# The two rounds of 32x32 products in a block inverse, spread over four cells of the matrix array

## The chip, the cores and the metric

The kernel runs on one core of a Trainium2 chip. That core has TensorE (PE: matmuls, and PEld for their weight loads), VectorE (DVE), ScalarE (ACT), GpSimd (POOL) and SyncE (SP), which issues the transfers. The metric is device time of one execution in microseconds (us). Before the change three runs took 1629.48 to 1632.38 us, median 1632.25 us.

## The reference: what is computed

The reference is a two-layer encoder trunk of width 1024, applied with one set of weights to a prompt of 512 tokens and a sample of 256. Layer 0 is a Mamba-2 mixer, layer 1 an RWKV-7 time mix; each is followed by a residual sum and a layer norm. The part that matters here is the recurrence of the second layer, for 16 heads of size 64, forward and backward in time:

```python
def step(s, inp):
    r_t, w_t, k_t, v_t, kk_t, a_t = inp
    sa = jnp.einsum('bhvk,bhk->bhv', s, -kk_t)
    s = (s * w_t[:, :, None, :] + sa[..., None] * (kk_t * a_t)[:, :, None, :]
         + v_t[..., None] * k_t[:, :, None, :])
    return s, jnp.einsum('bhvk,bhk->bhv', s, r_t)
```

The kernel doesn't step through the tokens. It takes chunks of 64 tokens. Inside a chunk the rank-one terms `sa` depend on each other through a triangular 64x64 matrix, and the chunk is solved with the inverse of one plus that matrix.

## The kernel before

Everything is float32. The large products are each made of three fp32r matmuls, a high and a low half of each operand (L140, L141, L142); they are called dense matmuls here.

Layer 1 is worked through in 8 blocks `b` of two heads. For each block there are four pieces:

- `rwkv_in(b)`: dense projections of the block's channels (PE, with ACT and DVE shifting and splitting; L737, L739, L122, L123).
- `p1(b)`: from the projections, per window of four chunks, the triangular matrices of the chunks. They land in `TD` (L914). A block has 24 units (6 windows of 4 chunks), and each unit holds two heads: head 0 in partitions 0 to 63, head 1 in 64 to 127.
- `rwkv_inverse(b)`: replaces the triangular matrices by the inverses, described below.
- `chain_step(b, 0..7)`: the eight dependent steps along the sequence, with small 64x64 matmuls (`pr`, `pS`, `pz` at L1017, `py` at L1039). The product `pS` of step 0 is the first to read the inverses.

`rwkv_inverse` treats each 64x64 triangle as 32x32 quarters. The two diagonal quarters of all units and heads are inverted together by forward substitution on VectorE: 30 pairs of a product (L963) and a sum (L964), each needing the one before. Two transposes (L966, L967) then give the inverted diagonal quarters in two layouts, `XN` and `XR`. What remains is the off-diagonal quarter, -2 times a product of three 32x32 matrices. It takes two rounds of 48 matmuls, 24 units by 2 heads:

- Round 1 (L977) multiplies the off-diagonal quarter of `TD` with `XN`. Its operands lie in the first 32 partitions of the head (`q0`), and the result is put in the second 32 (`q1`), so two cells of the array are used: row strip 0 with column strip 1, and row strip 2 with column strip 3. The results lie in the PSUM tile `tl`. ScalarE scales them into `E` in SBUF (L979; the profile names that buffer `TL`). This happens in two groups, units 0 to 15 and then 16 to 23; the second group's matmuls write the same PSUM tile that the first group's copy reads, and stand behind that copy.
- Round 2 (L986) multiplies `E` in `q1` with `XR` in `q1` into PSUM tile `px` at `q0`, again on two cells (row strips 1 and 3).
- ScalarE writes the diagonal quarters into `TD` (L982, four instructions), and the last four copies (L989) bring the off-diagonal quarters from `px` into `TD`, head 0 on VectorE and head 1 on ScalarE, each in two pieces (16 units and 8).

The order of the work isn't that of the code. `arrange` builds the dependencies of the whole program and hands them to a list scheduler with a cost for each instruction; the order it finds on each engine is fixed with ordering edges. A change in one place can therefore move instructions everywhere in the program, in layer 0 too.

Of the kernel before, what the change touches and what calls it, by code (L numbers as in the profile page):

```python
# [18 lines left out]
AF = mybir.ActivationFunctionType  # L19
# [29 lines left out]
def bc(ap, axis, n):  # L49
    a = ap.unsqueeze(axis)  # L50
    s = list(a.shape)
    s[axis] = n
    return a.to_broadcast(s)
# [6 lines left out]
class Trunk:  # L60
# [880 lines left out]
    def rwkv_inverse(self, b):  # L941


        nc = self.nc
        TD, XR, TS, XN = self.TD, self.TC, self.TL, self.XN
        hm = self.halfm
        spans = [(slice(u, u + n), slice(o, o + n)) for u, o, n in self.spans(b)]
        fl = lambda t: t.rearrange("p a b -> p (a b)")
        sw = lambda t: t.rearrange("p a b -> p b a")

        TL = self.pt("s", [P, 32, 32], "tl")
        for us, rs in spans:
            nc.scalar.activation(TL[:, us], TD[:, rs, 0, 0:32], AF.Copy, scale=hm[:, 2:3])
            nc.vector.scalar_tensor_tensor(TL[:, us], TD[:, rs, 0, 32:64], hm[:, 3:4], TL[:, us], op0=ALU.mult, op1=ALU.add)
        nc.vector.memset(TL[:, 24:], 0.0)
        nc.vector.transpose(TS, sw(TL))
        nc.scalar.copy(TL, TS)
        nc.vector.memset(fl(TL)[:, ::33], 1.0)
        tmp = fl(XN)
        for j in range(1, 31):  # L960
            m = 31 - j
            t = tmp[:, 0 : m * j].rearrange("p (a b) -> p a b", b=j)
            nc.vector.tensor_tensor(t, bc(TS[:, j + 1 : 32, j], 2, j), bc(TL[:, j, 0:j], 1, m), op=ALU.mult)  # L963
            nc.vector.tensor_add(TL[:, j + 1 : 32, 0:j], TL[:, j + 1 : 32, 0:j], t)  # L964

        nc.vector.transpose(XN, sw(TL))  # L966
        nc.vector.transpose(XR, TL)  # L967
        XN, XR = sw(XN), sw(XR)
        qs = [(slice(64 * h, 64 * h + 32), slice(64 * h + 32, 64 * h + 64)) for h in range(2)]
        E = TS  # L970
        groups = (slice(0, 16), slice(16, 24))
        place = [o + i for _, o, n in self.spans(b) for i in range(n)]
        ps = TL
        for g in groups:
            for u in range(24)[g]:
                for q0, q1 in qs:
                    nc.tensor.matmul(ps[q1, u, :], TD[q0, place[u], 0, 32:64], XN[q0, u, :], start=True, stop=True)  # L977

            nc.scalar.activation(E[:, g], ps[:, g], AF.Copy, scale=-2.0)  # L979
        for us, rs in spans:  # L980
            for i in range(2):
                nc.scalar.activation(TD[:, rs, 0, 32 * i : 32 * i + 32], XR[:, us], AF.Copy, scale=hm[:, i : i + 1])  # L982
        ps = self.pt("s", [P, 32, 32], "px")
        for u in range(24):
            for q0, q1 in qs:
                nc.tensor.matmul(ps[q0, u, :], E[q1, u, :], XR[q1, u, :], start=True, stop=True)  # L986
        for us, rs in spans:
            for h, (q0, q1) in enumerate(qs):
                (nc.vector.tensor_copy if h == 0 else nc.scalar.copy)(TD[q0, rs, 0, 32:64], ps[q0, us])  # L989

    def sv_load(self, b, step):

# [937 lines left out]
```

## Time and profile before

| | before |
|---|---|
| median of the runs | 1632.25 us |
| the profiled execution's own time | 1634.65 us |
| its span, first to last instruction | 1632.9 us |
| PE, DVE busy share of the span | 93%, 83% |
| PE busy in round 1 and in round 2, all 8 inverses | 24.5 us, 23.2 us |
| layer 1, from its first inverse to its last | 893 to 1549 us of the span |

Times in the views count from the first instruction of the span. An fp32 matmul of this size shows as two records, so 48 matmuls are 96 records. Rows of the timeline give start, length, engine, line, operation, names and the number of records merged.

### The profile page before, as it was taken

The page shows a single profiled execution, that of the slowest core. Times are in us where ns is not written, and L with a number is a line of the kernel's source. Part 1 is how long each engine was busy: PE and PEld are TensorE (multiplying, and loading weights), DVE is VectorE, ACT ScalarE, POOL GpSimd, SP SyncE. Part 2 cuts the span into 40 slices and gives each one's busy share as a digit, 9 for nine tenths or more (in the row PEclk, how much of TensorE's full clock was granted, in tenths as well). Part 3 has the DMA queues.
Part 4 walks back from the last instruction along what each step waited for, and adds up shares of the span by engine and source line. Part 5 has one row for each costly group of instructions (what it writes and reads, how often), then busy time and mean ns, then how long its engine had stood idle before and what let it go on. Part 6 is the DMA issues. An engine that isn't in the chain of part 4 may idle for free. (4 is left out here: it accounts for less than half of the span.)

```text
span 1632.9 us, 39446 instructions
## 1 busy us (share of the span) xinstructions
PE 1526.4 (93%) x15210; PEld 1293.0 (79%) x15210; DVE 1361.9 (83%) x3031; ACT 850.8 (52%) x1980; POOL 723.5 (44%) x1007
## 2 busy tenths in 40 slices
PE   7999999999999899999979989999898999988996
PEld 6888888888988689998758767777777777776885
DVE  6779988888888885668688898989989898989768
ACT  4345444544545352424464757657574757656332
POOL 1168465574574661000070836446372836547210
PEclk9999999999999899999988898999899999979998
DMA  5110211212112044513334343443434344354332
GB/s 175 54 47 26 78 40 59 72 65 72 56 36 85 13 143 143 182 53 110 120 109 132 94 122 107 116 140 101 139 88 126 113 121 126 102 159 137 97 111 85
DMA packets 150316, 161.41 MB, mean 99 GB/s; under 512 B 39632, under 2 KB 106928, under 8 KB 150128
## 3 DMA queue, kind: packets, MB, share of 16 engines
q1 hardware_dynamic: 150128, 158.89, 32.5%
q8 instruction: 120, 1.97, 0.5%
q14 instruction: 68, 0.56, 0.1%
HBM read 121.43 MB, written 40.55 MB: 99 GB/s over the span
## 5 line engine op out<-in xcount | busy, mean ns | idle before, releaser
L140 PE MATMUL pj<-xh,whi 128*128 128x256 f32 (+1 forms) x1056 | 384.7, 365 | 18.9 <-ACT whi L122 10.2
L142 PE MATMUL pj<-xh,wlo 128*128 128x256 f32 (+1 forms) x1056 | 381.1, 361 | 4.3 <-DVE wlo L123 4.3
L141 PE MATMUL pj<-xl,whi 128*128 128x256 f32 (+1 forms) x1056 | 378.3, 358 | 1.4 <-DVE xl L136 1.4
L140 PEld LDWEIGHTS pj<-xh,whi 128*128 128x128 f32 x1056 | 207.0, 196 | 50.6 <-ACT whi L122 10.3
L142 PEld LDWEIGHTS pj<-xh,wlo 128*128 128x128 f32 x1056 | 207.3, 196 | 30.6 <-DVE wlo L123 6.2
L141 PEld LDWEIGHTS pj<-xl,whi 128*128 128x128 f32 x1056 | 207.7, 197 | 27.0 <-DVE xl L136 2.0
L122 ACT CAST whi<-wraw 128x512 fp32r<-128x512 f32 x213 | 131.4, 620 | 125.2 <-PE pj L141 61.7
L123 DVE TENSOR_TENSOR wlo<-wraw,whi 128x512 fp32r<-128x512 f32 x213 | 159.9, 755 | 33.3 <-ACT whi L122 31.1
L414 POOL TENSOR_SCALAR G<-past,ddt,dt 128x128 f32<-128x128 f32 x192 | 136.2, 720 | 84.6 <-DVE ddt L320 57.8
L140 PE MATMUL po<-whi,xh 128*128 128x256 f32 x528 | 151.8, 288 | 1.5 <-DVE acc L501 1.5
L142 PE MATMUL po<-whi,xl 128*128 128x256 f32 x528 | 152.0, 288 | 0.0
L141 PE MATMUL po<-wlo,xh 128*128 128x256 f32 x528 | 151.5, 287 | 0.0
L234 DVE SCALAR_TENSOR_TENSOR conv<-conv,convw 128x770 f32<-128x770 f32 x128 | 140.7, 1099 | 1.3
L140 PE MATMUL pz<-whi,xh 128*128 128x256 f32 x384 | 113.9, 297 | 1.1 <-DVE sz L258 1.1
L378 POOL TENSOR_TENSOR xw<-xB,dtws 128x256 f32<-128x256 f32 x64 | 53.5, 845 | 135.8 <-ACT xB L366 126.3
L901 POOL TENSOR_TENSOR G<-EP,Wr 64x256 f32<-64x256 f32 x96 | 88.5, 922 | 56.7 <-DMA Wr<-ind 36.3
L142 PE MATMUL pz<-whi,xl 128*128 128x256 f32 x384 | 111.5, 290 | 0.0
L141 PE MATMUL pz<-wlo,xh 128*128 128x256 f32 x384 | 111.1, 290 | 0.0
L140 PEld LDWEIGHTS po<-whi,xh 128*128 128x128 f32 x528 | 100.8, 191 | 2.9 <-DVE acc L501 1.9
L141 PEld LDWEIGHTS po<-wlo,xh 128*128 128x128 f32 x528 | 100.9, 191 | 1.5 <-issue 0.3
L142 PEld LDWEIGHTS po<-whi,xl 128*128 128x128 f32 x528 | 100.6, 191 | 1.5 <-DVE xl L136 0.2
L903 POOL TENSOR_TENSOR G<-EP,Wr 64x256 f32<-64x256 f32 x96 | 89.4, 931 | 1.7 <-ACT KB L919 0.8
(274 smaller groups left out, 3837.9 us busy)
## 6 DMA issues: line engine op xcount, KB each, us to landing
wraw<-in_r_w_in SPq DMA_DIRECT2D x72, 256.0 KB
Wr<-ind SPq DMA_DIRECT2D x48, 384.0 KB
wraw<-in_m_w_xbc SPq DMA_DIRECT2D x64, 256.0 KB
wraw<-in_m_w_z SPq DMA_DIRECT2D x32, 256.0 KB
wraw<-in_m_w_out SPq DMA_DIRECT2D x32, 256.0 KB
ydram<-yst SPq DMA_DIRECT2D x16, 384.0 KB
yraw<-ydram SPq DMA_DIRECT2D x24, 256.0 KB
ind<-k SPq DMA_DIRECT2D x32, 192.0 KB
```

Source lines behind the costliest of these rows:

```text
L122: nc.scalar.copy(hi, raw)
L123: nc.vector.tensor_sub(lo, raw, hi.bitcast(F32))
L140: mm(ps, ah, bh, start=first, stop=False)
L141: mm(ps, ah, bl, start=False, stop=False)
L142: mm(ps, al, bh, start=False, stop=last)
L234: nc.vector.scalar_tensor_tensor(acc, u[:, t : t + n], w[:, b, t : t + 1], acc, op0=ALU.mult, op1=ALU.add)
L378: nc.gpsimd.tensor_tensor(hv(xw), hv(xB[c][:, 0:256]), bc(self.dtws[:, c, z, hs], 2, 64), op=ALU.mult)
L414: nc.gpsimd.tensor_scalar(G[:, h, :], self.past, self.ddt[:, c, i : i + 1], self.dt[:, c, 0, i : i + 1], op0=ALU.mult, op1=ALU.add)
L901: nc.gpsimd.tensor_tensor(G[hr, ps4, h, 0, :], EP[hr, :, 0:C], w4(tok(W[hr, h])), op=ALU.mult)
L903: nc.gpsimd.tensor_tensor(rho[..., ::-1] if z else rho, EP[hr, :, 1:], w4(tok(W[hr, 2])), op=ALU.mult)
```

## The change

Units 16 to 23 use another column strip than units 0 to 15. In round 1 their results land in `q0` where the others land in `q1`; in round 2 the other way round. The row strips stay, so each row strip now serves two neighbouring cells, one with 16 units and one with 8. The units are issued in the order 0, 16, 1, 2, 17, 3, ... (`mixed`).

Round 1 is one group now, followed by the copies. `E` is read in `q1` by round 2, so the copy of units 16 to 23 must bring them from `q0` to `q1`: it becomes two ScalarE copies of 32 partitions (one per head) in place of one of 128. That is 8 ScalarE instructions more over the 8 inverses. The last four copies keep their number and sizes; for units 16 to 23 they read `q1`.

```diff
-        groups = (slice(0, 16), slice(16, 24))
+        mixed = [u for i in range(8) for u in (2 * i, 16 + i, 2 * i + 1)]
         place = [o + i for _, o, n in self.spans(b) for i in range(n)]
         ps = TL
-        for g in groups:
-            for u in range(24)[g]:
-                for q0, q1 in qs:
-                    nc.tensor.matmul(ps[q1, u, :], TD[q0, place[u], 0, 32:64], XN[q0, u, :], start=True, stop=True)
-
-            nc.scalar.activation(E[:, g], ps[:, g], AF.Copy, scale=-2.0)
+        for u in mixed:
+            for q in qs:
+                nc.tensor.matmul(ps[q[u < 16], u, :], TD[q[0], place[u], 0, 32:64], XN[q[0], u, :], start=True, stop=True)
+        nc.scalar.activation(E[:, 0:16], ps[:, 0:16], AF.Copy, scale=-2.0)
+        for h, (q0, q1) in enumerate(qs):
+            nc.scalar.activation(E[q1, 16:24], ps[q0, 16:24], AF.Copy, scale=-2.0)
 ...
-        for u in range(24):
-            for q0, q1 in qs:
-                nc.tensor.matmul(ps[q0, u, :], E[q1, u, :], XR[q1, u, :], start=True, stop=True)
-        for us, rs in spans:
-            for h, (q0, q1) in enumerate(qs):
-                (nc.vector.tensor_copy if h == 0 else nc.scalar.copy)(TD[q0, rs, 0, 32:64], ps[q0, us])
+        for u in mixed:
+            for q in qs:
+                nc.tensor.matmul(ps[q[u >= 16], u, :], E[q[1], u, :], XR[q[1], u, :], start=True, stop=True)
+        for i, (us, rs) in enumerate(spans):
+            for h, q in enumerate(qs):
+                (nc.vector.tensor_copy if h == 0 else nc.scalar.copy)(TD[q[0], rs, 0, 32:64], ps[q[i], us])
```

The scheduler's order changes with it. Three places show how, all in the third of the 8 inverses. First TensorE, between the two rounds. Before:

```order
L977 MATMUL tl<-XN,TD 32x32 x32
L141 MATMUL pj_12396<-xl,whi 128x256
...
L141 MATMUL pj_13462<-xl,whi 128x512
L1104 MATMUL pf<-ident,Y 128x128 x2
L977 MATMUL tl<-XN,TD 32x32 x16
L142 MATMUL pj_13462<-xh,wlo 128x512
L140 MATMUL pj_13462<-xh,whi 128x512
L986 MATMUL px<-TC,TL 32x32 x48
```

and after:

```order
L976 MATMUL tl<-XN,TD 32x32 x48
L141 MATMUL pj_13465<-xl,whi 128x512
L142 MATMUL pj_13465<-xh,wlo 128x512
L140 MATMUL pj_13465<-xh,whi 128x512
L141 MATMUL pj_13465<-xl,whi 128x512
L142 MATMUL pj_13465<-xh,wlo 128x512
L140 MATMUL pj_13465<-xh,whi 128x512
L141 MATMUL pj_13465<-xl,whi 128x512
L986 MATMUL px<-TC,TL 32x32 x48
```

Round 1 stands in one piece, with one stretch of dense matmuls behind it instead of two. Second ScalarE, from the diagonal quarters to the copies of round 1. Before:

```order
L982 ACTIVATE TD<-TC,halfm 128x16x32
L982 ACTIVATE TD<-TC,halfm 128x8x32
L979 ACTIVATE TL<-tl 128x512
L982 ACTIVATE TD<-TC,halfm 128x16x32
L122 CAST whi<-wraw 128x512
L737 ACTIVATE g<-pj_12396,omu 128x256
L979 ACTIVATE TL<-tl 128x256
```

and after:

```order
L982 ACTIVATE TD<-TC,halfm 128x16x32
L982 ACTIVATE TD<-TC,halfm 128x8x32 x2
L977 ACTIVATE TL<-tl 128x512
L979 ACTIVATE TL<-tl 32x256 x2
L982 ACTIVATE TD<-TC,halfm 128x16x32
```

One of the 128x8x32 writes of diagonal quarters now stands ahead of the copies into `E`, and the three copies follow each other. Third VectorE, around the end of the forward substitution (L963, L964) and the two transposes. Before:

```order
L963 TENSOR_TENSOR XN<-TL,tl 128x58
L964 TENSOR_TENSOR tl<-tl,XN 128x2x29
L963 TENSOR_TENSOR XN<-TL,tl 128x30
L964 TENSOR_TENSOR tl<-tl,XN 128x30
L1114 TENSOR_TENSOR o<-o,sg 128x256
L966 STREAM_TRANSPOSE XN<-tl 128x1024
L809 SCALAR_TENSOR_TENSOR k<-rb,rpar,k 128x768
L967 STREAM_TRANSPOSE TC<-tl 128x1024
L739 SCALAR_TENSOR_TENSOR g<-pj_12371,hmu,g 128x511
L123 TENSOR_TENSOR wlo<-wraw,whi 128x512
L739 SCALAR_TENSOR_TENSOR g<-pj_12371,hmu,g 128x511
```

and after:

```order
L739 SCALAR_TENSOR_TENSOR g<-pj_12373,hmu,g 128x511
L963 TENSOR_TENSOR XN<-TL,tl 128x58
L739 SCALAR_TENSOR_TENSOR g<-pj_12373,hmu,g 128x511
L964 TENSOR_TENSOR tl<-tl,XN 128x2x29
L963 TENSOR_TENSOR XN<-TL,tl 128x30
L123 TENSOR_TENSOR wlo<-wraw,whi 128x512
L964 TENSOR_TENSOR tl<-tl,XN 128x30
L966 STREAM_TRANSPOSE XN<-tl 128x1024
L967 STREAM_TRANSPOSE TC<-tl 128x1024
```

Two shift sums (L739) and a weight split (L123) have moved from behind the transposes to ahead of them.

## The prediction

> **What bounds the kernel now.** I read the busy shares first, then busy time by stretches, then the timeline around one inverse.
>
> ```profile
> PE 1526.4 (93%) x15210; PEld 1293.0 (79%) x15210; DVE 1361.9 (83%) x3031; ACT 850.8 (52%) x1980; POOL 723.5 (44%) x1007
> 0.00:860.00 860.00, 818.52 (x6050) 717.80 (x6051) 686.86 (x1377) 396.16 (x847) 370.19 (x482) 0.98 0.27 83
> 1048.00:1079.00 31.00, 26.41 (x190) 21.58 (x190) 30.20 (x91) 13.61 (x32) 6.42 (x7) 0.94 0.40 119
> 1079.00:1092.00 13.00, 12.88 (x219) 10.86 (x220) 9.30 (x15) 9.36 (x17) 5.83 (x6) 0.87 0.63 195
> 1092.00:1144.00 52.00, 51.37 (x781) 40.09 (x780) 47.59 (x103) 39.51 (x107) 36.99 (x61) 1.00 0.35 101
> 1171.30:1183.50 12.20, 12.20 (x219) 10.08 (x217) 10.07 (x13) 10.10 (x22) 9.92 (x14) 0.86 0.52 157
> 1266.00:1279.50 13.50, 13.44 (x219) 11.03 (x217) 9.62 (x14) 9.80 (x20) 10.04 (x14) 0.75 0.60 191
> 1356.60:1368.50 11.90, 11.90 (x221) 10.04 (x219) 9.64 (x13) 9.91 (x21) 9.15 (x10) 0.86 0.57 168
> ```
>
> In the rows of stretches the columns are the length, busy time of PE, PEld, DVE, ACT, POOL, then granted TensorE clock, DMA share and GB/s. Layer 0 (first row) holds none of the changed work. In layer 1 a block takes some 90 us and has three stages. In the forward substitution (1048 to 1079) VectorE is busy for 30.20 of 31.00 us and sets the time. In the chain steps (1092 to 1144) TensorE is, for 51.37 of 52.00. Between them lies what I call the tail, from the second transpose to the first `pS`: 13.0, 12.2, 13.5 and 11.9 us in the four blocks shown. There PE is full, VectorE leaves 3.7, 2.1, 3.9 and 2.3 us idle (mean 3.0), and the clock falls to 0.75 to 0.87. Nothing of the chain can start before the tail ends, so its length counts; the change works inside it. This is the tail of the third inverse:
>
> ```profile
> 1079.12 1.98 PE L977 MATMUL tl<-XN,TD 32*32 32x32 f32 x64 [0.20 <-DVE TC L967]
> 1083.21 1.07 PE L977 MATMUL tl<-XN,TD 32*32 32x32 f32 x32
> 1084.88 2.89 PE L986 MATMUL px<-TC,TL 32*32 32x32 f32 x96
> 1092.00 0.68 PE L1017 MATMUL pS<-R,TD 64*64 64x64 f32 x16
> 1081.15 0.60 ACT L979 ACTIVATE TL<-tl 128x512 f32<-128x512 f32 x1
> 1084.33 0.38 ACT L979 ACTIVATE TL<-tl 128x256 f32<-128x256 f32 x1 [0.56 <-PE tl L977]
> 1084.61 0.73 ACT L982 ACTIVATE TD<-TC,halfm 128x256 f32<-128x256 f32 x1
> 1089.69 0.67 DVE L989 COPY TD<-px 32x512 f32<-32x512 f32 x1
> 1088.60 1.17 DVE L904 TENSOR_TENSOR KB<-KB,ld 128x512 f32<-128x512 f32 x1
> 1091.28 0.41 DVE L989 COPY TD<-px 32x256 f32<-32x256 f32 x1 [0.32 <-ACT TD L989]
> 1090.67 0.58 ACT L989 COPY TD<-px 32x512 f32<-32x512 f32 x1
> 1092.01 0.36 ACT L989 COPY TD<-px 32x256 f32<-32x256 f32 x1
> ```
>
> Round 1 starts 0.05 us after the transpose and round 2 ends at 1087.77: 8.65 us, of which the array works 1.98 + 1.07 + 2.89 = 5.94 us on the rounds. The rest is dense work put between, and two handovers to ScalarE.
>
> **The rounds themselves.** Each round has 48 matmuls, 24 per cell; 16 per cell (64 records) take 1.98 us and 24 (96 records) 2.89. So one more matmul on a cell costs (2.89 - 1.98)/8 = 0.114 us. After the change the busiest cells hold 16. If neighbouring cells of one row strip run beside each other, both rounds take 1.98 us, and an inverse needs 3.96 us of the array, 1.98 less; 8 inverses, 15.8 us less. The trace has no 32x32 products on neighbours, but it has 64x64 ones:
>
> ```profile
> 909.94 0.45 PE L1039 MATMUL py<-SV,TD 64*64 64x64 f32 x8
> 940.98 0.45 PE L1017 MATMUL pS<-R,TD 64*64 64x64 f32 x8
> 821.91 1.10 PE L912 MATMUL ptd<-G,KB 64*64 64x128 f32 x32 [1.11 <-POOL EP L880]
> ```
>
> Four `py` products share one row strip and alternate between its two column strips; four `pS` products go to two diagonal cells, which share nothing. Both take 0.45 us. L912 cycles through all four 64x64 cells. What it would need on two cells follows from `pS`: two products per cell take 0.45 us and four (the row at 1092.00) 0.68, so one more costs 0.115 us for 64 columns, 0.23 for L912's 128; 8 in a row would be over 1.8 us. Its 16 products take 1.10. So neighbours run together and I take the full gain. The other bound is no gain, 2.89 us a round.
>
> [...]
>
> **The handover.** Before, the second group of round 1 stood behind the first copy, and round 2 behind the second. After, one group is followed on ScalarE by one L982 of 128x256 (0.73, moved ahead), the copy of 128x512 (0.60) and two copies of 32x256 (not in the trace; the nearest row is L989's copy out of PSUM of that shape, 0.36 each; below, nothing, if it hid; above, the 0.60 of the wide copy). Sum 2.05 us, and I add 0.2 for handovers. Round 2 needs the last of them, since unit 16 is its second. From the start of round 1 to the end of round 2: 1.98 + 2.05 + 0.2 + 1.98 = 6.2 us in place of 8.65, that is 2.4 less. With both bounds of the small copies it is 1.9 to 3.2 less. The 8 ScalarE instructions more (8 x 0.36 = 2.9 us) lie on an engine that is busy half the time; they count through this chain alone. Behind them wait the last L982 and p1's activations, which nothing needs before the last copies.
>
> The four last copies are unchanged (0.67 + 0.58 + 0.41 + 0.36 in turn, since all read one PSUM tile), and in the tail shown the first of them came 1.9 us after round 2's end, behind VectorE's L904.
>
> **What VectorE lets through.** A tail shorter by 2.4 us is worth that only if the other work done in it still fits. Dense work has room: PE idles 4.6 us in the substitution stage. VectorE does not: what leaves the tail goes into the substitution, where it has 0.8 us left. The third inverse shows it, with two L739 and one L123 moved ahead of the transposes:
>
> ```profile
> 1078.99 0.71 DVE L739 SCALAR_TENSOR_TENSOR g<-pj,hmu,g 128x511 f32<-128x511 f32 x1
> 1080.61 0.74 DVE L739 SCALAR_TENSOR_TENSOR g<-pj,hmu,g 128x511 f32<-128x511 f32 x1
> 1083.43 0.69 DVE L123 TENSOR_TENSOR wlo<-wraw,whi 128x512 fp32r<-128x512 f32 x1 [1.75 <-ACT whi L122]
> ```
>
> That is 2.1 us of VectorE work which lengthens the substitution as far as it shortens the tail. So the net gain of a tail is the idle time of VectorE that goes away: at most the 3.0 us of the four rows, at least nothing. I take 1.75 us, between the 2.4 of the chain and half of the idle.
>
> **The clock.** The stretch that holds round 2 is followed by one at half clock:
>
> ```profile
> 1084.45:1087.87 3.42, 3.42 (x99) 2.96 (x99) 1.79 (x4) 1.63 (x3) 1.12 (x2) 1.00 1.04 353
> 1087.87:1091.28 3.41, 3.41 (x9) 2.64 (x10) 3.10 (x4) 2.23 (x6) 3.33 (x3) 0.50 0.36 135
> 1176.60:1180.03 3.43, 3.43 (x100) 2.97 (x99) 3.43 (x5) 2.82 (x8) 3.28 (x4) 1.00 0.11 27
> 1180.03:1183.44 3.41, 3.41 (x12) 2.59 (x12) 2.57 (x5) 2.30 (x6) 2.85 (x6) 0.50 0.65 187
> ```
>
> PE counts as busy throughout, but 2.89 of 3.42 us were 32x32 products. With rounds of 1.98 us there is room for 1.4 us of dense work in such a stretch, and some of the half-clock stretches should go. Each would give back up to 3.41/2 = 1.7 us of dense work. I count none of it in the sum, since VectorE limits what the tail can give; it widens the range downwards. [...]
>
> **The sum.** 8 inverses x 1.75 = 14 us less than the profiled execution's 1634.65 (span 1632.9 and 1.75 around it): 1620.65. That execution lies 2.4 us above the median of the runs, so against the runs the forecast is 1632.25 - 14 = 1618.25, 1618 us.
>
> **Rivals.**
> 1. The tail gives all (14 in 100): 3.0 us each, VectorE's whole idle time, with the clock kept: 24 us less, 1608. For it: the clock stands at 0.75 in the tail at 1266, so there is more to win than in the one worked out. Against: VectorE has to wait for each round whatever its length, so some idle stays.
> 2. VectorE takes it back (12 in 100): the moved 2.1 us lengthen the substitution, and the chain's 2.4 are nearly cancelled; 0.4 us each, 3 less, 1629. For it: 30.20 of 31.00. Against: the tail has 3.0 us of idle VectorE time that needs no payment.
> 3. The neighbours take turns, so the change doesn't do what it says (8 in 100): rounds of 2.89, from start to end 2.89 + 2.25 + 2.89 = 8.0 in place of 8.65, with the array's work as before: 0 to 0.6 us each, 1627 to 1632. For it: at 32x32 no row shows neighbours. Against: `py`.
> 4. Slower (8 in 100): VectorE's moved work lengthens the substitution by 2.1 us or more in seven blocks, and the tail doesn't shorten, because behind round 2 the four last copies still stand between VectorE's other work, as they did at 1089.69. If the tails give less than 2.1 us it turns to a loss; with 1.0 given, 8 x 1.1 = 9 us more, 1641. Against: the three rows that moved stood behind the transposes before, so VectorE is freer when round 2 ends.
>
> **How the numbers follow.** The forecast holds 58 in 100, from 1612 to 1625 by itself. Within 0.2% (3.3 us) a measurement of this kernel can't tell a change from none. Rivals 2 and 3 lie on both sides of that bound; I count 8 of their 20 as faster and 12 as within. Faster: 58 + 14 + 8 = 80 in 100. Within: 12. Slower: 8. The range, 1608 to 1630, leaves out the lower half of rival 1 (7), the upper part of rival 3 (5) and rival 4 (8).
>
> **What would show it.** In the changed kernel, both rounds as runs of 96 records in 1.9 to 2.1 us (right) or near 2.9 (rival 3). PE busy in the rounds, 24.5 + 23.2 us before, at about 32. Round 1's start to round 2's end near 6.2 us. Tails of 9.5 to 11.5 us with VectorE idle for 1 to 2 us, and forward-substitution stages longer by no more than what left the tail; if they are longer by over 2 us with tails as long as now, rival 4. Layer 0 should end within 2 us of where it did; if it moves by more, the new order there, and not the inverse, decides, and the sum above is wrong in its place even where the total fits.

## The result and the profile after

The changed kernel takes 1614.92 us (median of 4 runs, 1611.99 to 1616.7) against 1632.32 us before on the same chip: a ratio of 0.9894, 95% interval 0.9873 to 0.9914, or 17.3 us less. The forecast was 1618. The profiled execution took 1611.99 us, its span 1610.2 us. Medians and ratios in this document are over fast runs: two runs of long_plan_mixed (1694.6 and 4674.4 us) and one of the kernel before (1837.5 us) were slow and are left out.

First the busy shares of the changed kernel, then its fourth inverse in the timeline of TensorE and ScalarE (start, length, engine, line, names, records).

```profile
PE 1497.8 (93%) x15210; PEld 1270.9 (79%) x15210; DVE 1353.2 (84%) x3031; ACT 853.3 (53%) x1988; POOL 717.6 (45%) x1007
```

```profile
1162.92 2.01 PE L976 MATMUL tl<-XN,TD 32*32 32x32 f32 x96
1167.12 2.00 PE L986 MATMUL px<-TC,TL 32*32 32x32 f32 x96
1164.90 0.79 ACT L982 ACTIVATE TD<-TC,halfm 128x256 f32<-128x256 f32 x1 [0.30 <-PE tl L976]
1165.58 0.58 ACT L977 ACTIVATE TL<-tl 128x512 f32<-128x512 f32 x1
1166.18 0.76 ACT L979 ACTIVATE TL<-tl 32x256 f32<-32x256 f32 x2
```

Both rounds take 2.0 us with their 96 records, where 24 products on one cell took 2.89. Round 1 starts at 1162.92 and round 2 ends at 1169.12, 6.2 us. Between them ScalarE works its queue as the order had it: 0.79 us for the write of diagonal quarters, 0.58 for the wide copy and 0.76 for the two narrow ones together.

The stages, summed over the program. The rows are sums over the 8 tails (second transpose to first `pS`), the 8 forward substitutions and the 7 chains between, first of the kernel before, then of the changed one; the first figure is the length, then busy time by engine.

```profile
sum 109.80, PE 107.85 PEld 91.74 DVE 74.99 ACT 81.75 POOL 65.06; mean PE 13.48 PEld 11.47 DVE 9.37 ACT 10.22 POOL 8.13
sum 322.60, PE 282.97 PEld 229.46 DVE 304.46 ACT 146.06 POOL 72.92; mean PE 35.37 PEld 28.68 DVE 38.06 ACT 18.26 POOL 9.12
sum 263.90, PE 254.56 PEld 199.04 DVE 237.95 ACT 205.28 POOL 208.42; mean PE 36.37 PEld 28.43 DVE 33.99 ACT 29.33 POOL 29.77
```

```profile
sum 72.00, PE 67.30 PEld 57.14 DVE 57.58 ACT 66.40 POOL 46.42; mean PE 8.41 PEld 7.14 DVE 7.20 ACT 8.30 POOL 5.80
sum 330.50, PE 293.54 PEld 237.41 DVE 313.75 ACT 154.11 POOL 82.18; mean PE 36.69 PEld 29.68 DVE 39.22 ACT 19.26 POOL 10.27
sum 273.10, PE 253.22 PEld 200.82 DVE 239.89 ACT 212.48 POOL 217.03; mean PE 36.17 PEld 28.69 DVE 34.27 ACT 30.35 POOL 31.00
```

The tails lost 37.8 us. The substitutions took 7.9 of them back and the chains 9.2. VectorE's idle time (length less DVE) fell by 20.4 us in the tails, from 34.8 to 14.4, and rose by 7.3 in the chains. Layer 0 ended where it did: VectorE's memset that opens the first inverse starts at 852.9 us before and 852.4 after.

TensorE gives a second account of the same difference. Its busy and idle time add up to the span in every run, so the account sorts a difference and doesn't by itself name a cause. Its busy time fell by 1526.4 - 1497.8 = 28.6 us. The rounds' rows, all 8 inverses together, show 16.0 and 16.1 us where they showed 24.5 and 23.2, which makes 15.6 of it:

```profile
L986 PE MATMUL px<-TC,TL 32*32 32x32 f32 x768 | 16.1, 230 | 1.4 <-ACT TL L979 1.4
L976 PE MATMUL tl<-XN,TD 32*32 32x32 f32 x768 | 16.0, 227 | 4.2 <-DVE TC L967 4.2
```

The other 13.0 us are other matmuls, as many as before, done in less time: the time under half clock (the granted clock is 1.00 or 0.50 in the two traces, nothing else) fell from 130.6 to 94.5 us. (Of either figure, 2.0 us lie behind the last instruction.) Against that TensorE idles 5.9 us more (112.4 us for 106.5). 15.6 + 13.0 - 5.9 = 22.7 us, the difference of the two spans. The medians differ by less, 17.3 us, since the profiled execution of before lay above its median and that of after below it.

### The profile page after: what moved, and what is told of

The parts are those of the page before. It is cut to its first block, busy times and chain, and to the rows that moved or that the text cites. A ratio compares the mean times of both kernels' runs of the same rounds, so it can differ in the third digit from the quotient of the medians.

```text
span 1610.2 us, 39447 instructions
## 1 busy us (share of the span) xinstructions
PE 1497.8 (93%) x15210; PEld 1270.9 (79%) x15210; DVE 1353.2 (84%) x3031; ACT 853.3 (53%) x1988; POOL 717.6 (45%) x1007
## 4 chain that ended last, share of the span: by engine, by line
PE 65%; DVE 17%; ACT 6%; POOL 5%; DMA 3%; issue 3%; SPq 0%; DVEq 0%; POOLq 0%; ACTq 0%
PE pj L140 9%; PE pj L142 9%; PE pj L141 9%; PE po L141 3%; PE po L142 3%; PE po L140 3%; PE ptd L912 3%; PE pz L140 3%; PE pz L141 3%; PE pz L142 3%; PE py L1039 3%; DVE tl L964 2%; DVE XN L963 2%; PE pst L380 2%; PE py L419 2%
## 5 line engine op out<-in xcount | busy, mean ns | idle before, releaser
L140 PE MATMUL pj<-xh,whi 128*128 128x512 f32 (+1 forms) x1056 | 382.1, 362 | 21.5 <-ACT whi L122 11.4
L142 PE MATMUL pj<-xh,wlo 128*128 128x512 f32 (+1 forms) x1056 | 372.7, 353 | 2.4 <-DVE wlo L123 2.4
L141 PE MATMUL pj<-xl,whi 128*128 128x512 f32 (+1 forms) x1056 | 371.9, 352 | 1.2 <-DVE xl L136 1.2
L142 PEld LDWEIGHTS pj<-xh,wlo 128*128 128x128 f32 x1056 | 203.6, 193 | 28.6 <-DVE wlo L123 4.2
L141 PEld LDWEIGHTS pj<-xl,whi 128*128 128x128 f32 x1056 | 204.3, 193 | 24.5 <-DVE xl L136 1.8
L123 DVE TENSOR_TENSOR wlo<-wraw,whi 128x512 fp32r<-128x512 f32 x213 | 155.6, 735 | 30.0 <-ACT whi L122 28.4
L414 POOL TENSOR_SCALAR G<-past,ddt,dt 128x128 f32<-128x128 f32 x192 | 127.6, 674 | 77.3 <-DVE ddt L320 57.3
L378 POOL TENSOR_TENSOR xw<-xB,dtws 128x256 f32<-128x256 f32 x64 | 52.8, 834 | 131.1 <-ACT xB L366 122.9
```

Of the source, the lines that this page charges most:

```text
L123: nc.vector.tensor_sub(lo, raw, hi.bitcast(F32))
L140: mm(ps, ah, bh, start=first, stop=False)
L141: mm(ps, ah, bl, start=False, stop=False)
L142: mm(ps, al, bh, start=False, stop=last)
L378: nc.gpsimd.tensor_tensor(hv(xw), hv(xB[c][:, 0:256]), bc(self.dtws[:, c, z, hs], 2, 64), op=ALU.mult)
L414: nc.gpsimd.tensor_scalar(G[:, h, :], self.past, self.ddt[:, c, i : i + 1], self.dt[:, c, 0, i : i + 1], op0=ALU.mult, op1=ALU.add)
```

## The experiments

Twelve kernels were run. One table for all of them, as the text comes back to it: array time of both rounds, TensorE's busy and idle time, time under half clock (each from the one profiled execution, in us), the mean granted clock over all runs of the kernel (lowest to highest), the median, and the ratio to the kernel before on the same chip with its interval.

| kernel | rounds | PE busy | PE idle | half clock | clock of the runs | median | ratio |
|---|---|---|---|---|---|---|---|
| before | 47.7 | 1526.4 | 106.5 | 130.6 | 0.954 to 0.968 | 1632.3 | 1 |
| changed | 32.1 | 1497.8 | 112.4 | 94.5 | 0.971 to 0.974 | 1614.9 | 0.9894 (0.9873 to 0.9914) |
| order_only | 42.9 | 1529.0 | 119.5 | 151.5 | 0.955 to 0.962 | 1640.1 | 1.0046 (1.0026 to 1.0065) |
| one_group | 46.4 | 1520.7 | 108.6 | 134.4 | 0.956 to 0.963 | 1632.8 | 1.0008 (0.9994 to 1.0022) |
| round1_only | 39.2 | 1508.6 | 117.4 | 106.8 | 0.962 to 0.969 | 1629.8 | 0.9990 (0.9975 to 1.0004) |
| round2_only | 40.5 | 1505.2 | 114.5 | 90.1 | 0.968 to 0.975 | 1625.4 | 0.9951 (0.9933 to 0.9969) |
| replan_before | 47.7 | 1519.6 | 114.8 | 129.5 | 0.953 to 0.961 | 1638.4 | 1.0045 (1.0030 to 1.0060) |
| replan_after | 32.1 | 1511.2 | 115.8 | 142.3 | 0.952 to 0.961 | 1628.4 | 0.9982 (0.9971 to 0.9994) |
| late_neighbours | 32.9 | 1508.2 | 110.1 | 113.2 | 0.966 to 0.973 | 1617.7 | 0.9918 (0.9898 to 0.9938) |
| even_split | 25.8 | 1506.0 | 116.4 | 131.1 | 0.959 to 0.964 | 1622.7 | 0.9953 (0.9936 to 0.9970) |
| after_plan_long_rounds | 42.9 | 1515.5 | 107.3 | 108.2 | 0.967 to 0.974 | 1621.4 | 0.9932 (0.9914 to 0.9951) |
| long_plan_mixed | 32.1 | 1514.4 | 123.9 | 139.8 | 0.957 to 0.965 | 1634.5 | 1.0014 (0.9995 to 1.0032) |
| before_plan_round2 | 40.5 | 1510.5 | 115.6 | 102.0 | 0.961 to 0.971 | 1626.6 | 0.9953 (0.9928 to 0.9979) |
| after_plan_late | 32.1 | 1501.9 | 109.6 | 98.6 | 0.970 to 0.974 | 1613.8 | 0.9888 (0.9866 to 0.9909) |

One execution isn't the kernel: the runs of one kernel differ in their mean clock by up to 0.014, and 0.01 of it is some 33 us under half clock (an estimate: 2 x 0.01 x 1630, with the clock at 0.50 in that time). So the half-clock and busy columns are to be read beside the clock of the runs. For order_only and long_plan_mixed the profiled execution had a clock (0.955 and 0.958) at the low end of its runs, and order_only's, with 1650.4 us, was the slowest of its ten.

My theory was that the neighbours run side by side and that the shorter tails set the gain. Against it stood first that the removed handover is all of it, and second that the array's time is hidden.

### Units in turn: order_only

```diff
-        mixed = [u for i in range(8) for u in (2 * i, 16 + i, 2 * i + 1)]
+        mixed = list(range(24))
```

> The changed kernel with one thing undone: the units are issued 0 to 23 in turn, so that units 16 to 23 come last instead of between the others. Cells, copies and the single group stay. Theory (neighbours run side by side, and the length of the rounds is what pays): TensorE takes its work in order, so the 16 units of the first cell hold back the 8 of its neighbour; rounds of 2.8 to 2.9 us instead of 2.0, round 1's start to round 2's end near 8.0 us, and half or more of the gain is lost: 1621 to 1628 us. Rival (the gain is the removed second handover alone, since dense work fills the rest): rounds longer all the same, but the time stays at 1615 within 3 us. Second rival (a row strip passes one product at a time and the rounds got short for another reason): the rounds stay at 2.0 us.

This is round 1 of its third inverse, and then the rows of both rounds over all 8 inverses:

```profile
1079.70 2.67 PE L976 MATMUL tl<-XN,TD 32*32 32x32 f32 x96
```

```profile
L986 PE MATMUL px<-TC,TL 32*32 32x32 f32 x768 | 21.5, 229 | 2.3 <-ACT TL L979 2.3
L976 PE MATMUL tl<-XN,TD 32*32 32x32 f32 x768 | 21.4, 228 | 5.6 <-DVE TC L967 5.6
```

The rounds got longer by 0.67 us each, to 2.67, not to the 2.8 to 2.9 I expected. So the neighbours do run beside each other, for 24 products on one cell took 2.89, but the full saving, 2.0 us, came only with their products beside each other in the order. The time was a miss for the theory and for both rivals: 1640 us, 8 above the kernel before, though its rounds are shorter than that kernel's. Something else moved by more than the rounds. One place is plain: the memset that opens the first inverse stands at 861.2 us here, 8.3 later than before, in a part of the program where nothing of the change lies. The scheduler had built another order for everything: in the traces the sequence of VectorE parts from that of the changed kernel at the 13th instruction. How much of the 8.3 us that order makes is less plain, for long_plan_mixed below has the same order and that memset at 856.7 us.

### One group on two cells: one_group

```diff
+        for u in range(24):
+            for q0, q1 in qs:
+                nc.tensor.matmul(ps[q1, u, :], TD[q0, place[u], 0, 32:64], XN[q0, u, :], start=True, stop=True)
         for g in groups:
-            for u in range(24)[g]:
-                for q0, q1 in qs:
-                    nc.tensor.matmul(ps[q1, u, :], TD[q0, place[u], 0, 32:64], XN[q0, u, :], start=True, stop=True)
-
             nc.scalar.activation(E[:, g], ps[:, g], AF.Copy, scale=-2.0)
```

> The kernel before with round 1 in one group: all 48 products first, then the two copies of 128 partitions. Two cells as before, no neighbours, no copies of 32 partitions. Theory (both the handover and the length of the rounds pay): rounds of 2.9 us, start of round 1 to end of round 2 at 2.9 + 1.2 + 2.9 = 7.0 to 7.7 us in place of 8.65, and 1622 to 1628 us. Rival (the handover is all of it): 1615 within 3 us. Rival (only array time counts): no change from before, 1632 within 3 us.

No change: 1.0008 (0.9994 to 1.0022). These are its tails and its chains, summed as above:

```profile
sum 94.10, PE 84.94 PEld 74.07 DVE 69.24 ACT 71.83 POOL 57.87; mean PE 10.62 PEld 9.26 DVE 8.66 ACT 8.98 POOL 7.23
sum 269.90, PE 258.56 PEld 206.34 DVE 231.28 ACT 205.81 POOL 207.69; mean PE 36.94 PEld 29.48 DVE 33.04 ACT 29.40 POOL 29.67
```

The tails did get shorter, by 15.7 us in sum (109.8 to 94.1), yet the chains gave 6.0 back and the part ahead of the first inverse 4.1. VectorE's idle time shows where the gain went: 9.9 us of it left the tails (34.8 to 24.9) and 12.7 more came in the chains (25.95 to 38.62). So a shorter tail isn't by itself a gain, and VectorE idle that leaves the tail isn't one either. That contradicts my own expectation (1622 to 1628) and the rival of the handover; the rival "only array time counts" fits.

The handover itself did get shorter. From the start of round 1 to the end of round 2 it takes 6.95 to 7.08 us in three of the inverses, as expected, and 8.6 to 10.0 in the other five. Less the array time of the rounds that is 2.8 us on average, against 3.5 before and 2.6 in the changed kernel. So it has most of the shorter handover, and in this order nothing of that shows in the time.

### Neighbours in one round: round1_only, round2_only

The first has the changed kernel's round 1 with the round 2 of before; the second the reverse. The heart of the second, against the kernel before (its last copies change with it, as in the change above):

```diff
 ...
-        for u in range(24):
-            for q0, q1 in qs:
-                nc.tensor.matmul(ps[q0, u, :], E[q1, u, :], XR[q1, u, :], start=True, stop=True)
+        for u in mixed:
+            for q in qs:
+                nc.tensor.matmul(ps[q[u >= 16], u, :], E[q[1], u, :], XR[q[1], u, :], start=True, stop=True)
 ...
```

> Neighbours in round 1 alone; round 2 and its copies as before. Theory: round 1 at 2.0 us, round 2 at 2.9, start to end near 7.1 us, and more than half of the gain, since the single group comes with it: 1618 to 1624 us. Rival (handover alone): 1615 within 3 us, as the changed kernel. Rival (the new plan and not the rounds): anything between 1610 and 1635, without order by the length of the rounds.

> Neighbours in round 2 alone; round 1 in its two groups on two cells, with its two copies, as before. Theory: round 1 at 3.06 us, round 2 at 2.0, start to end near 7.8 us in place of 8.65, 0.9 us less in each of 8 tails: 1624 to 1629 us. Rival (the handover alone pays): 1632 within 3 us. Rival (the clock: round 2 is what brings the half-clock stretch behind it): half-clock time in the tails falls as far as in the changed kernel, from 49 us to some 22, and the time to 1620 or less.

Round 1 alone came to 1629.8 us, 0.9990 (0.9975 to 1.0004), no change and a miss; round 2 alone to 1625.4, 0.9951, as expected. By the array's time the first should have given more (8.5 us to 7.2). The rival of the clock was half right in the second: half clock in the tails fell to 13.7 us, further than asked for, but the time did not reach 1620. In the table they differ in the clock, 106.8 us at half clock to 90.1, and in the part ahead of the first inverse, which ends at 859.1 us in the one and 851.7 in the other. Both can be matters of the order, so by now the order had to be measured for itself.

### What another order does: replan_before, replan_after

```diff
-DMA_NS = 1700
+DMA_NS = 1720
```

> The kernel before, computing the same with the same instructions; only one number that the list scheduler assumes (the fixed time of a transfer) goes from 1700 to 1720, so that it settles on another order of the whole program. It measures what another order of equal merit does to the time. Theory (the rounds' length and the clock behind it set the gain of the change, and the order scatters the time by some us): 1632 within 8 us. Rival (the order is all of it: the changed kernel was lucky): some 10 us or more away from 1632.

> The changed kernel with the same small change of the scheduler's number, 1700 to 1720, and so another order. Theory: 1615 within 8 us, and 10 us or more below the kernel before under its own new order. Rival (a lucky order): it falls back to 1625 to 1632 us.

Another order moves the kernel before by +0.45% (7 us), and the changed one from 0.9894 to 0.9982, 14 us. Both were expected within 8 us; the second was not, so the scatter is larger than the theory allowed. replan_before also shows again that the length of the tails decides nothing by itself: its tails are 17 us shorter than those of before (92.7 to 109.8, summed as above), and it is the slower one. The pair under new orders still differs by 10 us (1638.4 to 1628.4), but with a scatter of this size a single pair of orders can't tell what the rounds are worth. The table says what the order does: replan_after has all of the rounds' saving in TensorE's busy time (1511.2, 15.2 below before) and nothing of the clock's, 142.3 us at half clock in place of 94.5. All its runs agree on that: their clock is 0.952 to 0.961, that of the changed kernel 0.971 to 0.974.

### The order held fixed

The last four kernels take the order of the whole program as a list that was found for another kernel, the same on every engine, instruction by instruction (the lists themselves are not shown):

```diff
-    for line in prog.schedule().values():
+    for line in map(fixed, PLAN):
 ...
```

In the traces the sequence on VectorE, ScalarE and GpSimd is the same, instruction by instruction, as that of the kernel whose order was taken.

after_plan_long_rounds has the changed kernel's order with the units in turn; long_plan_mixed has the order of order_only with the mixed units; before_plan_round2 has the order of the kernel before with round 2 on four cells.

> The changed kernel's order of the whole program, held fixed on every engine (written into the kernel instead of searched), with the units of both rounds issued 0 to 23 in turn. So nothing differs from the changed kernel but the length of the rounds, 2.67 us (as that order of units gave before) in place of 2.0. Theory (the length of the rounds sets the gain, the order scatters it): 2 x 0.67 us in each of 8 inverses, 10.7 us of array time, and some half-clock time back: 1623 to 1632 us. Rival (the order is the gain): 1615 within 3 us.

> The opposite corner: the order of the whole program of the run with units in turn (1640 us), held fixed, with the units in the changed kernel's mixed order, so that the rounds take 2.0 us. Theory: 8 to 17 us below 1640, 1623 to 1632 us, and what then remains above 1615 is the worth of the order. Rival (the order is all): 1640 within 3 us.

> The order of the kernel before, held fixed, with round 2 alone on four cells: the same instructions in the same places, round 2 at 2.0 us in place of 2.89. Theory: 0.9 us in each of 8 inverses, 7.1 us, and less half-clock time behind round 2: 1618 to 1625 us against 1631. Rival (in the order made for long rounds a shorter one only makes TensorE wait for the copies): 1631 within 3 us.

These are the clean comparisons. In the changed kernel's order, 10.8 us of array time (42.9 to 32.1) are worth 0.9932 - 0.9894, 6 us (2 to 11, with the two intervals taken as independent). In the order of order_only the same 10.8 us are worth 1.0046 - 1.0014, 5 us (1 to 10). In the order of before, 7.2 us of round 2 are worth 1 - 0.9953, 8 us (3 to 12). The first two fell short of what I expected (8 to 17 us); the rival that the order is all failed in the first and third, and in the second the intervals meet. after_plan_late, described below, supports the first: on the same chip, in the same order and with rounds of 2.0 us, its runs took 1611.1 to 1618.5 us against 1619.0 to 1624.6.

On the other side, at 42.9 us of rounds the two orders differ by 1.0046 - 0.9932, 19 us, and at 32.1 by 1.0014 - 0.9894, 20 us. So the order weighs more than the rounds. The changed code has now run in three orders, at 0.9894, 0.9982 and 1.0014, and the code of before in two, at 1 and 1.0045: the changed kernel's own order is the best of its three. And with its rounds made long again it still stands at 0.9932, so 11 of its 17 us don't hang on the last 10.8 us of array time; the order, the single group and the 4.8 us of array time that are left (47.7 to 42.9) share them in parts that no run tells apart.

The tails of after_plan_long_rounds, summed:

```profile
sum 82.50, PE 78.80 PEld 69.12 DVE 60.17 ACT 69.30 POOL 49.97; mean PE 9.85 PEld 8.64 DVE 7.52 ACT 8.66 POOL 6.25
```

82.5 us where the changed kernel has 72.0, so with one order 10.8 us of array time lengthen the tails by 10.5, and nearly nothing of it comes back: the substitutions are 2.3 us longer and the chains 2.1 shorter. Between the profiled executions 12.6 us arrive in the span, but these are the slowest of the one kernel's four runs and the fastest of the other's; by the medians it is 6. So shorter rounds do shorten the tail, and with the order fixed the program gets shorter with it.

In before_plan_round2 the third and fourth tails show the clock. The columns are those of the prediction's rows of stretches; the last three are granted clock, DMA share and GB/s.

```profile
1076.80:1088.60 11.80, 10.72 (x221) 8.79 (x221) 8.60 (x13) 8.68 (x16) 5.31 (x5) 1.00 0.67 213
1166.10:1177.20 11.10, 10.87 (x227) 8.85 (x225) 9.80 (x12) 10.28 (x22) 8.33 (x9) 1.00 0.57 173
```

Their clock was 0.87 and 0.86 before; with a shorter round 2 as the only change it is 1.00 in both. The kernel's half-clock time falls by 28.6 us in all (130.6 to 102.0), and TensorE's busy time by 15.9, of which 7.2 are the rounds. Over all runs on that chip the median clock goes from 0.963 in the kernel before to 0.969, some 20 us of half clock by the estimate above. Against that TensorE idles 9.1 us more, so the rival, that it would wait, holds in part.

### Two versions meant to be faster: late_neighbours (and with the order held, after_plan_late), even_split

late_neighbours puts the neighbours of round 2 behind, so that its start doesn't need the narrow copies; even_split gives 12 units to each cell.

```diff
-        for u in mixed:
+        for u in [*range(8), *(u for i in range(8) for u in (8 + i, 16 + i))]:
             for q in qs:
                 nc.tensor.matmul(ps[q[u >= 16], u, :], E[q[1], u, :], XR[q[1], u, :], start=True, stop=True)
```

```diff
-        mixed = [u for i in range(8) for u in (2 * i, 16 + i, 2 * i + 1)]
+        mixed = [u for i in range(12) for u in (i, 12 + i)]
...
-                nc.tensor.matmul(ps[q[u < 16], u, :], TD[q[0], place[u], 0, 32:64], XN[q[0], u, :], start=True, stop=True)
+                nc.tensor.matmul(ps[q[u < 12], u, :], TD[q[0], place[u], 0, 32:64], XN[q[0], u, :], start=True, stop=True)
...
```

> The changed kernel with another order of the units in round 2 alone: 0 to 7 first, then 8, 16, 9, 17, ... 15, 23. The busiest cell still has 16 units, so the round keeps 2.0 us, but its first third doesn't need the two copies of 32 partitions and can start 0.7 us earlier. Theory (the tail's length sets the time): 0.5 us less in each of 8 tails, 1611 us, if the order of the program doesn't scatter more than that. Rival (what ends the tail is the work around the rounds): 1615 within the scatter of the order.

> The changed kernel's order held fixed, with round 2's units in the order 0 to 7, 8, 16, 9, 17, ... 15, 23, so that its first third doesn't need the two copies of 32 partitions. Theory (the tail's length sets the time): 0.3 to 0.7 us less in each of 8 tails, 1610 to 1613 us. Rival (TensorE has dense work ahead of round 2 in its order, so round 2 starts when that is done, and not when the copies are): 1615 within 2 us.

> The changed kernel with the units shared evenly: 12 on each of the two cells of a row strip instead of 16 and 8. The copies become one of 128x384 and two of 32x384, and in every other block two more small copies of 4 units bring the results back. Theory (array time pays): rounds of 1.5 to 1.6 us, 0.9 us less array time in each inverse, the wide copy shorter by 0.1 and the two narrow ones longer by 0.1 each: 1609 to 1614 us. Rival (below 2 us a round, the copies and VectorE bound the tail): 1615 within 4 us.

With the order held, the late neighbours come to 0.9888 (0.9866 to 0.9909), not to be told from the changed kernel; the rival fits, for in that order round 2 stands behind dense matmuls, and TensorE idles only 1.4 us ahead of it in all 8 inverses of the changed kernel. Under an order of its own it is 0.9918, 7 us above what I expected. Neither is a better version. The even split has a round 1 of 1.55 us and the shortest tails of all, 64.3 us in sum, and yet is 0.6% (10 us) behind the changed kernel, outside of what the theory and the rival allowed:

```profile
L986 PE MATMUL px<-TC,TL 32*32 32x32 f32 x768 | 13.4, 229 | 9.5 <-ACT TL L979 7.6 <-issue 1.8
L976 PE MATMUL tl<-XN,TD 32*32 32x32 f32 x768 | 12.4, 228 | 0.5 <-DVE TC L967 0.5
```

Of the 9.5 us of idle time ahead of round 2, 7.6 are TensorE waiting for the copies, and round 2 itself takes 1.56 to 3.69 us. Its chains are 20 us longer than the changed kernel's (293.4 to 273.0), with 57.1 us of half clock in them for 15.7. How much of that is the split and how much its order, no run here tells apart.

## Why the prediction was right, and where it was not

**The rounds.** Right, in size too. 16 deep was forecast at 1.98 us and measured 2.00; the saving at 15.8 us of array time, measured 15.6. That the neighbours in a row strip run together was read from 64x64 products; it held at 32x32. Had the neighbours taken turns, a round would have stayed near 2.9 us; the trace shows 2.0, and 1.55 with 12 and 12. order_only adds what the order does to it: with the units in turn, so that the products of the two cells didn't stand beside each other, a round took 2.67.

**The handover.** The size was right (6.2 us from round to round forecast, 5.9 to 7.8 measured, six of eight between 5.9 and 7.1; the narrow copies 0.37 each for 0.36). That it would pay was not shown: one_group has most of it and gains nothing in its order.

**What VectorE lets through.** This is the step that failed in its reason. I took 1.75 us a tail as the VectorE idle time that would go away, and argued that VectorE takes back what leaves the tail. The size of that idle time was misread to begin with: the four rows had a mean of 3.0 us, two of them started 1 to 2 us behind the transpose, and over all 8 tails it is 34.8/8 = 4.4 us. It fell to 1.8, and the tails to 9.0 us on average, below the 9.5 to 11.5 that I had forecast. The tails did give up 37.8 us, of which 17.1 came back in substitutions and chains, so something takes it back, and the moved VectorE work is part of it: the substitutions hold 9.3 us more of it and are 7.9 longer. But the net gain isn't the VectorE idle that leaves the tails. That fell by 9.9 us in one_group, 16.4 in replan_before and 25.3 in even_split, for no gain, a loss of 7 us and a gain of 8 (0.9953), because 12.7, 14.5 and 20.0 us of idle came into the chains, which the sum left out. In the changed kernel it was 20.4 against 7.3. Net, a tail gave 17.3/8 = 2.2 us by the medians; the term was low by a fifth, and stood for something else.

**The clock.** I counted none of it in the sum. That was the mis-sized term: 13.0 of the 28.6 us by which TensorE's busy time fell between the two profiled executions are other matmuls, with 36 us less under half clock. That a shorter round 2 takes half-clock time away was right where it could be seen alone: in before_plan_round2, with nothing else moved, the third and fourth tails have a clock of 1.00 in place of 0.87 and 0.86.

**What the sum left out.** The order of the rest of the program. I took it into account only as a check on layer 0, which passed (0.5 us), and that check was too weak, since between kernels with one and the same order that memset moved by 1.7, 2.1 and 4.5 us. But the scheduler's order is worth 7 to 20 us at the same instructions, as much as the whole change, and no rival carried it. So the forecast of 14 us was right for the total of a pair, partly by luck, and can't be claimed for the inverse alone: with the order held fixed, array time was worth 0.5 to 1.1 us for each us saved (0.1 to 1.6 by the intervals), which for 15.6 us is 8 to 17. What of the 17.3 us beyond that is a luckier order stays open; the changed code in the order of before can't be run, since its round 1 has other instructions.

Of the rivals, the third (neighbours take turns) and the fourth (slower) are refuted. The first, all of VectorE's idle time, did not come: 14.4 of 34.8 us stayed in the tails. The second, that work comes back elsewhere, happened to nearly half of the tails' gain.

## What to carry to other kernels

Small fp32 products ran beside each other in neighbouring cells here, in one row strip too, when the issue order alternated between the cells, and the depth of the fullest cell gave the price of the round: 48 products of 32x32 took 2.89 us with 24 on it, 2.0 with 16 and 1.55 with 12, and 2.67 with 16 but the units in turn. Where a scheduler orders the whole program, hold its order fixed to learn what a change is worth, or run several orders: a cost assumption moved by 1% was worth 7 and 14 us here, against 17 for the change. And a stage that gets shorter is no gain until the stages behind it are added up: in one_group, replan_before and even_split the chains got longer by 6, 8.5 and 29 us.

## What the runs showed that I had not expected

With the units in turn, a round took 2.67 us, not 2.89. The 24 products of a row strip in strict succession would take what they took on one cell, 2.89; the 0.22 us between are the time of about two products (an estimate, at 0.114 each). Which products ran beside each other in such a round was not shown.

The clock also fell where the profile has TensorE busy all the time. In the traces of the kernel before and of the changed one its changes lie whole multiples of 3.41 us apart. Cut into such stretches, the kernel before has 352 with a clock of 1.00 in which TensorE is busy for over 97%. Half clock follows 5 of them, those from 988.88, 1084.45, 1176.61, 1272.19 and 1360.93 us, and in these the 32x32 products of the rounds fill 2.58 to 2.89 of the 3.41 us; in the other 347 they fill 2.06 at most. The changed kernel has 349 such stretches, with at most 2.01 us of the rounds in one, and half clock follows none. What sets the clock was not shown. And most half-clock periods began elsewhere: of those that follow a full clock, 12 of 21 in the kernel before and 11 of 15 in the changed one stand behind a stretch in which TensorE is busy for under 60%.

One half-clock stretch of 3.41 us more or less is worth up to 1.7 us of dense work (an estimate, half of 3.41), and orders of the same instructions differ by 48 us in their half-clock time (94.5 in the changed kernel, 142.3 in replan_after). There it is most of what made one order better than the other: their busy time differs by 13.4 us, their idle time by 3.4. Between the changed kernel and long_plan_mixed, the same code in a third order, idle time counts for more: 16.6 us of busy time and 11.5 of idle.
